# A two-layer trunk: the second matrix product of both MLPs in another order of work

## The chip, the cores and the metric

One core of one Trainium2 chip runs the whole kernel as one launch. The metric is the device time of that launch in microseconds: the median of the runs of one kernel. Beside it stands one profiled execution, whose trace all views below come from.

## The reference, cut to what matters

Two layers, each a mixer and an MLP, over 1024 tokens of 1024 features. `sandwich` is put around each of the four sublayers; the MLPs are sublayers 1 and 3, and sublayer 3 is the last of the kernel.

```python
def rms_norm(x, w=None):
    y = x32 * lax.rsqrt(jnp.mean(x32 * x32, axis=-1, keepdims=True) + EPS)
    ...
def squared_relu_mlp(h, w1, w2):                 # w1: 1024 x 4096, w2: 4096 x 1024
    return jnp.square(jax.nn.relu(h @ w1)) @ w2

def sandwich(x, c_act, sublayer, g_pre, g_post, w_mod, b_mod):
    shift, scale, gate = jnp.split(c_act @ w_mod + b_mod, 3, axis=-1)
    h = rms_norm(x, g_pre) * (1 + scale[:, None]) + shift[:, None]
    return x + gate[:, None] * rms_norm(sublayer(h), g_post)
```

All of it is float32. The kernel makes each float32 product from three products of a shorter format: each operand is split into a high part (a cast) and a low part (what the cast left), and high x high, high x low and low x high are added.

## The kernel before

The MLP (`mlp`, L492) works in two stages. The first product (loop L590) makes the hidden activations feature by feature and stores seven combinations of their quarters to DRAM (`ud[1]` to `ud[7]`, each 16 feature tiles of 128 x 512). The second product multiplies them with combinations of the four quarters of `w2` (x11, x12, x21, x22; each 2048 x 512). It is a Strassen-Winograd scheme: seven products of half size in place of eight, and additions. The results are four quarters of the output: `top` holds the first 512 tokens (row tiles 0 to 3), `low` the last 512 (row tiles 4 to 7), each with two halves of 512 columns.

Before the change the second product (L655 to L736) is cut in two passes `c` over the features. A pass loads eight feature tiles of all four quarters of `w2` into SBUF (L676, 1 MB per load, in the four large buffers hh0, hl0, hh1, hl1). Then it makes the seven products in the order 1, 2, 5, 3, 6, 4, 7. A product takes four PSUM banks, one per row tile, and four steps `q` of two feature tiles; a step forms the difference of weights where needed (L684 to L689, VectorE), splits the weights (`split_w`: high part on ScalarE L156, low part on VectorE L158; a ring of four buffers) and the activations (`split_to`, L489 and L490; buffers from a ring of six), and issues 24 matmuls of 512 columns (L701 to L703). After a product's four steps the banks are emptied: in the first pass by a copy on ScalarE (L706), in the second by an addition on VectorE (L709), with the scheme's further additions behind it (L711 to L722).

A finished row tile goes through `post` (L384): squares summed on ScalarE (L390), the gain `gg` by GpSimd in two halves (L393; by VectorE for every fourth tile), reciprocal root (L133 on VectorE, L135 on GpSimd), and one VectorE instruction that scales it and adds the old `x` (L398), with a load of `x` before and a store behind. If another sublayer follows, `pre_norm` squares the new `x` (L380), and L382 normalizes it into `Y`; `hT_cols` transposes `Y` on TensorE (L414) and makes the high and low parts of the next sublayer's input (L416 to L418). Row tiles 0 to 3 are posted after product 6 of the second pass (L724), row tiles 4 to 7 after all products (L731). The next mixer begins with units that need only the first half of hT.

A scheduler orders the instructions of each engine when the kernel is built; on the chip every engine runs its own in that order. All loads and stores of this stage are issued on SyncE's queue, in order.

Of the kernel before, what the change touches and what calls it, by code (L numbers as in the profile page):

```python
# [9 lines left out]
F32 = mybir.dt.float32  # L10
F32R = mybir.dt.float32r
# [7 lines left out]
P = 128  # L19
D = 1024  # L20
# [8 lines left out]
def trunk(ctx: ExitStack, tc: tile.TileContext, x, c, rel_bias, norm_gains, mod_w, mod_b, mlp_w1, mlp_w2,  # L29
# [372 lines left out]

    def new_hT(hf):
        return tuple(hp.tile([P, 8, 512], F32R, tag=f"{n}{hf}", name=f"{n}{hf}") for n in ("hh", "hl"))
# [87 lines left out]
    def mlp(yp, s):  # L492
# [19 lines left out]
        with ExitStack() as st:  # L512
# [77 lines left out]
            for it in range(8):  # L590
# [68 lines left out]
        mid = [slot(t, pair, F32, "mid") for t in range(4)]  # L659
        five = [slot(4 + t, pair, F32, "five") for t in range(2)]  # L660
        acc = {1: [m[:, 0] for m in mid], 6: [m[:, 1] for m in mid], 2: [m[:, 0] for m in top], 3: [m[:, 1] for m in top],
               4: [m[:, 0] for m in low], 7: [m[:, 1] for m in low], 5: [five[t // 2][:, t % 2] for t in range(4)]}
# [3 lines left out]
        def u_slot():  # L666
            us_at[0] += 1
            return slot((8, 9, 10, 11, 6, 7)[us_at[0] % 6], pair, F32R, "u")

        for c in range(2):  # L670
            xs = {}
            for key, tag, j, n in ((11, "hh0", 0, 0), (21, "hl0", 1, 0), (12, "hh1", 0, 1), (22, "hl1", 1, 1)):
                xs[key] = hp.tile([P, 8, 512], F32, tag=tag, name="x")
                for h in range(2):
                    r0 = j * 2048 + c * D + h * 512
                    nc.sync.dma_start(out=xs[key][:, h * 4:h * 4 + 4],  # L676
                                      in_=w2[r0:r0 + 512, n * 512:n * 512 + 512].rearrange("(k p) n -> p k n", p=P))
            for i, key in ((1, 11), (2, 21), (5, 11), (3, 22), (6, 22), (4, 21), (7, 12)):
                ps = [bank() for _ in range(4)]
                for q in range(4):  # L680
                    ks = slice(q * 2, q * 2 + 2)
                    x11, x12, x21, x22 = (xs[k][:, ks] for k in (11, 12, 21, 22))
                    if i == 5:
                        tt(out=x11, in0=x12, in1=x11, op=sub)  # L684
                    elif i == 6:
                        tt(out=x12, in0=x22, in1=x12, op=sub)
                        tt(out=x22, in0=x22, in1=x11, op=sub)
                    elif i == 4:
                        tt(out=x21, in0=x21, in1=x22, op=sub)  # L689
                    wh, wl = split_w(pair, xs[key][:, ks])  # L690
                    if q % 2 == 0:
                        raw = wp.tile([P, 4, 512], F32, tag="raw", name="uraw", bufs=2)
                        k0 = c * 8 + q * 2
                        nc.sync.dma_start(out=raw, in_=ud[i][k0:k0 + 4].rearrange("k p n -> p k n"))
                    uh, ul = u_slot(), u_slot()
                    split_to(uh, ul, raw[:, q % 2 * 2:q % 2 * 2 + 2])
                    for t in range(4):
                        ts = slice(t * P, t * P + P)
                        for k in range(2):
                            first, last = q == 0 and k == 0, q == 3 and k == 1  # L700
                            mm(ps[t], lhsT=uh[:, k, ts], rhs=wh[:, k], start=first, stop=False)  # L701
                            mm(ps[t], lhsT=uh[:, k, ts], rhs=wl[:, k], start=False, stop=False)  # L702
                            mm(ps[t], lhsT=ul[:, k, ts], rhs=wh[:, k], start=False, stop=last)  # L703
                for t in range(4):
                    if c == 0:
                        nc.scalar.copy(out=acc[i][t], in_=ps[t])  # L706
                        continue
                    a = {n: v[t] for n, v in acc.items()}
                    tt(out=a[i], in0=ps[t], in1=a[i], op=add)  # L709
                    if i == 2:  # L710
                        tt(out=a[2], in0=a[1], in1=a[2], op=add)  # L711
                    elif i == 3:
                        tt(out=a[3], in0=a[5], in1=a[3], op=add)
                    elif i == 6:
                        tt(out=a[6], in0=a[1], in1=a[6], op=add)
                        tt(out=a[3], in0=a[6], in1=a[3], op=add)
                        tt(out=a[5], in0=a[6], in1=a[5], op=add)
                    elif i == 4:
                        tt(out=a[4], in0=a[6], in1=a[4], op=add)
                    elif i == 7:  # L720
                        tt(out=a[4], in0=a[7], in1=a[4], op=add)
                        tt(out=a[7], in0=a[5], in1=a[7], op=add)  # L722
                if c == 1 and i == 6:
                    for t in range(4):  # L724
                        x_new = post(yp, t, s, yp.Y[t])
                        if s != sub_last:
                            pre_norm(yp, t, x_new)
# [3 lines left out]
        for t in range(4):  # L731
            x_new = post(yp, 4 + t, s, slot(t, [P, D], F32, "yg"))
            if s != sub_last:
                pre_norm(yp, 4 + t, x_new)
# [802 lines left out]
```

## Time and profile before

| | us |
|---|---|
| median of three runs | 3067.3 |
| lowest and highest run | 3060.2 and 3067.34 |
| the profiled execution | 3064.09 |
| its span | 3062.1 |
| TensorE busy in the span | 2931.0 |
| VectorE busy | 2039.6 |
| ScalarE busy | 1327.1 |
| GpSimd busy | 489.0 |

The span reaches from the first to the last instruction of the core. The second product of the first MLP fills it from about 1430 to 1746 us, that of the second MLP from about 2720 to 3038 us. TensorE (PE) is matmul, PEld the load of its weights beside it, DVE is VectorE, ACT ScalarE, POOL GpSimd, SP SyncE. Busy time is a share of a stretch; what a stretch waits for is read from the bracket behind an instruction, which gives its engine's idle time just before it and who ended it.

### The profile page before, as it was taken

The numbers are of one execution on the slowest core, as the hardware profiler recorded it, in microseconds if no ns is written. First come the engines' busy times: TensorE is split into PE (matmuls) and PEld (weight loads), VectorE is DVE, ScalarE is ACT, GpSimd is POOL, SyncE is SP. The second block draws the span as 40 slices with busy tenths as digits, with TensorE's granted clock in tenths as the row PEclk, the third lists the DMA queues.
The fourth block names the chain that finished last, engine by engine and source line by source line (L and its number), as shares of the span: only waits on it lengthen the run. The fifth ranks groups of instructions, "written<-read, shape, count | busy, mean of one in ns | idle before, by whom it ended". The sixth has DMA issues, their size and how long they took to land.

```text
span 3062.1 us, 39916 instructions
## 1 busy us (share of the span) xinstructions
PE 2931.0 (96%) x15250; PEld 2471.6 (81%) x15250; DVE 2039.6 (67%) x3282; ACT 1327.1 (43%) x2372; POOL 489.0 (16%) x434
## 2 busy tenths in 40 slices
PE   8999989999999989999999889999999899999996
PEld 5878879888877868888888678989988688888885
DVE  5797885555686488867557845565454876675577
ACT  5233335555543264445443365432222654454432
POOL 0243543222200120000000432001101100000004
PEclk9999999999999999999999989999999999999998
DMA  6231312111132246647443442153232454474423
GB/s 212 74 102 56 111 48 64 48 56 49 41 146 104 76 144 242 210 143 274 138 163 97 131 126 63 32 169 110 82 139 90 138 179 165 152 268 151 151 97 124
DMA packets 250786, 380.03 MB, mean 124 GB/s; under 512 B 13801, under 2 KB 149602, under 8 KB 249698
## 3 DMA queue, kind: packets, MB, share of 16 engines
q1 hardware_dynamic: 250208, 377.36, 36.8%
q8 instruction: 120, 1.97, 0.3%
q14 instruction: 72, 0.59, 0.1%
q10 hardware_dynamic: 386, 0.11, 0.0%
HBM read 285.67 MB, written 91.75 MB: 123 GB/s over the span
## 4 chain that ended last, share of the span: by engine, by line
PE 80%; DVE 11%; DMA 4%; ACT 2%; issue 2%; POOL 1%; SPq 0%; DVEq 0%; ACTq 0%; POOLq 0%
PE pw L701 4%; PE pw L702 4%; PE pw L703 4%; PE pw L536 4%; PE pw L537 4%; PE pw L538 4%; PE pg L433 4%; PE pg L434 4%; PE pg L435 4%; PE pg L751 4%; PE pg L753 3%; PE pg L752 3%; PE pg L445 3%; PE pg L447 3%; PE pg L446 3%; PE pg L536 2%
## 5 line engine op out<-in xcount | busy, mean ns | idle before, releaser
L156 ACT CAST wh<-raw 128x1024 fp32r<-128x1024 f32 (+1 forms) x218 | 227.6, 1047 | 305.7 <-PE pw L537 99.0
L751 PE MATMUL pg<-wh,hh 128*128 128x256 f32 (+1 forms) x992 | 292.1, 295 | 15.8 <-DVE zs L786 11.4
L433 PE MATMUL pg<-hh,wh 128*128 128x512 f32 x736 | 292.1, 398 | 1.8 <-ACT hh L416 0.7
L434 PE MATMUL pg<-hl,wh 128*128 128x512 f32 x736 | 291.6, 396 | 0.5 <-DVE hl L418 0.3
L435 PE MATMUL pg<-hh,wl 128*128 128x512 f32 x736 | 291.8, 396 | 0.0
L753 PE MATMUL pg<-wh,hl 128*128 128x256 f32 (+1 forms) x992 | 287.6, 290 | 0.6 <-DVE hl L418 0.6
L752 PE MATMUL pg<-wl,hh 128*128 128x256 f32 (+1 forms) x992 | 288.0, 290 | 0.0
L158 DVE TENSOR_TENSOR wl<-raw,wh 128x1024 fp32r<-128x1024 f32 (+1 forms) x162 | 199.5, 1233 | 129.3 <-ACT wh L156 126.4
L490 DVE TENSOR_TENSOR u<-uraw,u 128x1024 fp32r<-128x1024 f32 x112 | 139.1, 1242 | 191.8 <-ACT u L489 191.0
L489 ACT CAST u<-uraw 128x1024 fp32r<-128x1024 f32 x112 | 117.2, 1048 | 311.0 <-PE pw L702 209.1
L701 PE MATMUL pw<-wh,u 128*128 128x512 f32 x608 | 241.0, 397 | 0.0
L702 PE MATMUL pw<-wl,u 128*128 128x512 f32 x608 | 240.4, 395 | 0.0
L703 PE MATMUL pw<-wh,u 128*128 128x512 f32 x608 | 239.4, 394 | 0.0
L751 PEld LDWEIGHTS pg<-wh,hh 128*128 128x128 f32 x992 | 193.6, 195 | 19.0 <-DVE zs L786 10.7
L135 POOL TENSOR_TENSOR rs<-ms,expo 128x1 f32<-128x1 f32 x160 | 108.1, 677 | 617.2 <-DVE ms L133 599.1
L753 PEld LDWEIGHTS pg<-wh,hl 128*128 128x128 f32 x992 | 193.1, 195 | 2.6 <-DVE hl L418 1.3
L752 PEld LDWEIGHTS pg<-wl,hh 128*128 128x128 f32 x992 | 193.4, 195 | 1.9 <-issue 0.5
L445 PE MATMUL pg<-wh,u 128*128 128x512 f32 x448 | 182.1, 407 | 3.6 <-DVE u L883 3.0
L393 POOL TENSOR_TENSOR top<-top,gg 128x512 f32<-128x512 f32 x12 | 29.7, 2500 | 965.2 <-ACT junk L390 965.2
L447 PE MATMUL pg<-wh,u 128*128 128x512 f32 x448 | 178.6, 399 | 0.0
L446 PE MATMUL pg<-wl,u 128*128 128x512 f32 x448 | 177.5, 396 | 0.0
L158 POOL TENSOR_TENSOR wl<-raw,wh 128x1024 fp32r<-128x1024 f32 x58 | 145.5, 2512 | 146.4 <-ACT wh L156 127.3
(462 smaller groups left out, 7443.1 us busy)
## 6 DMA issues: line engine op xcount, KB each, us to landing
uraw<-ud SPq DMA_DIRECT2D x56, 1024.0 KB, 5.4
x<-in_mlp_w_dram SPq DMA_DIRECT2D x32, 1024.0 KB, 7.4
raw<-in_mod_w_dram SPq DMA_DIRECT2D x24, 1024.0 KB, 5.0
ud<-sums SPq DMA_DIRECT2D x48, 512.0 KB, 4.3
raw<-in_mlp_w_dram SPq DMA_DIRECT2D x18, 1024.0 KB, 5.5
raw<-in_e_w_in_dram SPq DMA_DIRECT2D x32, 512.0 KB, 4.0
ud<-c SPq DMA_DIRECT2D x64, 256.0 KB, 2.5
mraw<-in_mod_w_dram SPq DMA_DIRECT2D x32, 512.0 KB, 5.1
```

Source lines behind the costliest of these rows:

```text
L158: lo_on[0].tensor_tensor(out=wl, in0=src, in1=wh.bitcast(F32), op=ALU.subtract)
L433: mm(ps, lhsT=wh[:, k], rhs=hh[:, k], start=(k == 0), stop=False)
L434: mm(ps, lhsT=wh[:, k], rhs=hl[:, k], start=False, stop=False)
L435: mm(ps, lhsT=wl[:, k], rhs=hh[:, k], start=False, stop=(k == 7))
L445: mm(ps, lhsT=uh[:, tl], rhs=wh[:, f % 2], start=(f == 0), stop=False)
L447: mm(ps, lhsT=ul[:, tl], rhs=wh[:, f % 2], start=False, stop=(f == 3))
L701: mm(ps[t], lhsT=uh[:, k, ts], rhs=wh[:, k], start=first, stop=False)
L702: mm(ps[t], lhsT=uh[:, k, ts], rhs=wl[:, k], start=False, stop=False)
L703: mm(ps[t], lhsT=ul[:, k, ts], rhs=wh[:, k], start=False, stop=last)
L751: mm(ps[:, 0:n], lhsT=hh[:, k, tl], rhs=wh[:, i], start=(k == 0), stop=False)
L752: mm(ps[:, 0:n], lhsT=hh[:, k, tl], rhs=wl[:, i], start=False, stop=False)
L753: mm(ps[:, 0:n], lhsT=hl[:, k, tl], rhs=wh[:, i], start=False, stop=(k == 7))
```

## The change

The two passes become one: each of the seven products runs over all 16 feature tiles (eight steps) in PSUM. The order is 1, 2, 6, 5, 3, 7, 4. Product 2 goes on in the banks of product 1, and product 3 in those of product 5, after a copy or an addition has read them. Per MLP 56 readings of a bank become 32, and the additions that followed them go away but for those listed.

The weights no longer lie in SBUF whole: a `Stream` loads a quarter of `w2` in eight pieces of 512 KB. W11 is kept over products 1, 6 and 5, W22 over 6 and 4; W21, W22 and W12 are loaded again for later products, W12 and the second W21 through two small buffers that take turns (`tags` is None). The ring for split activations grows from six to eight buffers.

Row tiles 0 to 3 are posted in product 7 (`finish`), and the first half of hT is made in the first half of product 4. That product's last four steps are held: their operands are split, and then their matmuls are issued row tile by row tile, 24 each, with the end of that tile behind it (`post_tail`). `half_sum` treats a half of a row tile: the square's sum on ScalarE, the gain on VectorE (first half) or GpSimd (second half, done ahead). The loads of `xt` go to buffers of their own.

```diff
+    def half_sum(yp, y, cc):
+        junk = yp.tmp.tile([P, 512], BF16, tag="junk", name="junk")
+        ss = stat.tile([P, 1], F32, tag=f"ssh{cc}", name="ssh")
+        nc.scalar.activation(junk, y, AF.Square, accum_out=ss)
+        (nc.gpsimd if cc else nc.vector).tensor_tensor(out=y, in0=y, in1=gg[:, cc * 512:cc * 512 + 512], op=ALU.mult)
+        return ss
+
+    def post_tail(yp, t, s, xt, ss1):
+        src = x[0].rearrange("(t p) d -> t p d", p=P) if s == subs[0] else xd[s - 1]
+        nc.sync.dma_start(out=xt, in_=src[t])
+        Y = yp.Y[t]
+        ss0 = half_sum(yp, Y[:, 0:512], 0)
+        nc.vector.tensor_tensor(out=ss0, in0=ss0, in1=ss1, op=ALU.add)
+        r = rstd_of(ss0, D)
+        nc.vector.scalar_tensor_tensor(out=xt, in0=Y, scalar=r, in1=xt, op0=ALU.mult, op1=ALU.add)
+        dst = out[0].rearrange("(t p) d -> t p d", p=P) if s == sub_last else xd[s]
+        nc.sync.dma_start(out=dst[t], in_=xt)
+        return xt
...
-            return slot((8, 9, 10, 11, 6, 7)[us_at[0] % 6], pair, F32R, "u")
-
-        for c in range(2):
...
-            for i, key in ((1, 11), (2, 21), (5, 11), (3, 22), (6, 22), (4, 21), (7, 12)):
...
+            return slot((8, 9, 10, 11, 4, 5, 6, 7)[us_at[0] % 8], pair, F32R, "u")
...
+            def step(self, q):
+                if self.tags is None:
+                    t = slot(2 + turn("x"), pair, F32, "x")
+                    nc.sync.dma_start(out=t, in_=self.src[q])
+                    return t
+                if q == len(self.kept):
+                    t = hp.tile([P, 4, 2, 512], F32, tag=self.tags[q // 4], name="x")
+                    for i in range(4):
+                        nc.sync.dma_start(out=t[:, i], in_=self.src[q + i])
+                        self.kept.append(t[:, i])
+                return self.kept[q]
+
+        h0, h1 = ("hh0", "hl0"), ("hh1", "hl1")
+
+        t1, t2_ = Stream(11, h0), Stream(22, h1)
+        plan = ((1, [t1]), (2, [Stream(21, h1)]), (6, [t2_, Stream(12, None), t1]), (5, [t1]), (3, [Stream(22, h0)]),
+                (7, [Stream(22, h0), Stream(12, None)]), (4, [Stream(21, None), t2_]))
...
+                if i == 4 and q >= 4:
+                    held.append((uh, ul, wh, wl))
+                else:
+                    products(ps, [(uh, ul, wh, wl)], range(4), q == 0 and i not in (2, 3), q == 7, more)
+                if i == 7 and q % 2:
+                    finish(q // 2, yp.Y[q // 2])
+                if i == 4 and s != sub_last and q < 4:
+                    if q == 0:
+                        hT[0] = new_hT(0)
+                    hT_cols(yp, 0, s + 1, hT[0], (2 * q, 2 * q + 1))
...
+            for t in range(4):
+                c11, c12, c21, c22 = top[t][:, 0], top[t][:, 1], low[t][:, 0], low[t][:, 1]
...
+                elif i == 7:
+                    tt(out=c22, in0=ps[t], in1=c22, op=add)
+                    tt(out=c21, in0=ps[t], in1=u2[t], op=add)
+                else:
+                    if t == 0:
+                        sums = [half_sum(yp, c22_, 1) for c22_ in (l_[:, 1] for l_ in low)]
+                    products(ps, held, (t,), False, True, more)
+                    tt(out=c21, in0=ps[t], in1=c21, op=add)
+                    x_new = post_tail(yp, t + 4, s, xts[t], sums[t])
+                    if s != sub_last:
+                        pre_norm(yp, 4 + t, x_new)
```

What the scheduler makes of it, first on TensorE at the end of the first MLP, before: `pht` is a bank for transposes, `top` row tiles 0 to 3, `pg<-hh,wh` a matmul of the next mixer's first unit.

```order
L702 MATMUL pw<-wl,u 128x512
L414 MATMUL pht<-kmat,top 128x128 x2
L703 MATMUL pw<-wh,u 128x512
L414 MATMUL pht<-kmat,top 128x128 x2
L433 MATMUL pg<-hh_14969,wh 128x512 x2
L414 MATMUL pht<-kmat,top 128x128 x4
L434 MATMUL pg<-hl_14970,wh 128x512
L435 MATMUL pg<-hh_14969,wl 128x512
```

The same place after the change (L740 to L742 are the product's matmuls, L435 the transposes, L454 to L456 the mixer's first unit; `low` is row tile 4):

```order
L740 MATMUL pw<-wh,u 128x512
L741 MATMUL pw<-wl,u 128x512
L742 MATMUL pw<-wh,u 128x512
L435 MATMUL pht<-kmat,low 128x128 x2
L454 MATMUL pg<-hh_14840,wh 128x512
L455 MATMUL pg<-hl_14841,wh 128x512
L456 MATMUL pg<-hh_14840,wl 128x512
```

The transposes of row tile 3 (`top`) and most of those for the first half of hT, which stood behind the last matmul and among the mixer's first unit, are among the matmuls of product 4 now; behind the last matmul stand two transposes of an earlier tile and the mixer's units.

On VectorE at the end of the kernel, before (numbers of buffers kept: low_23535 is row tile 7):

```order
L709 TENSOR_TENSOR low_23535<-pw_25497,low_23535 128x512
L721 TENSOR_TENSOR low_23534<-low_23534 128x512
L721 TENSOR_TENSOR low_23535<-low_23535 128x512
L133 TENSOR_SCALAR ms_25662<-ss_25658 128x1
L722 TENSOR_TENSOR low_23534<-five_23541,low_23534 128x512
L722 TENSOR_TENSOR low_23535<-five_23541,low_23535 128x512
L393 TENSOR_TENSOR yg_25684<-low_23535,gg_106 128x512
L398 SCALAR_TENSOR_TENSOR xt_25652<-yg_25642,rs_25650,xt_25652 128x1024
```

After (low_23524 and low_23525 are row tiles 6 and 7, L788 reads their banks):

```order
L788 TENSOR_TENSOR low_23524<-pw_25316,low_23524 128x512
L408 TENSOR_TENSOR low_23524<-low_23524,gg_106 128x512
L417 TENSOR_TENSOR ssh_25631<-ssh_25631,ssh_25523 128x1
L133 TENSOR_SCALAR ms_25635<-ssh_25631 128x1
L419 SCALAR_TENSOR_TENSOR xt_25512<-low_23524,rs_25637,xt_25512 128x1024
L788 TENSOR_TENSOR low_23525<-pw_25317,low_23525 128x512
L408 TENSOR_TENSOR low_23525<-low_23525,gg_106 128x512
L417 TENSOR_TENSOR ssh_25668<-ssh_25668,ssh_25527 128x1
L133 TENSOR_SCALAR ms_25672<-ssh_25668 128x1
L419 SCALAR_TENSOR_TENSOR xt_25513<-low_23525,rs_25674,xt_25513 128x1024
```

Before, all four last tiles were read, combined and scaled together behind the last matmul; now a tile is done whole before the next one's bank is read.

On VectorE between products 7 and 4 of the first MLP, after the change (pw_14405 and pw_14406 are product 7's banks of row tiles 4 and 5; `wl` the low part of a weight split):

```order
L511 TENSOR_TENSOR u_14923<-uraw_14920,u_14922 128x1024
L782 TENSOR_TENSOR low_12975<-pw_14405,low_12975 128x512
L783 TENSOR_TENSOR low_12975<-pw_14405,u2_12979 128x512
L158 TENSOR_TENSOR wl_14918<-x_14913,wh_14916 128x1024
L731 TENSOR_TENSOR x_14968<-x_14968,x_13545 128x1024
L782 TENSOR_TENSOR low_12976<-pw_14406,low_12976 128x512
L783 TENSOR_TENSOR low_12976<-pw_14406,u2_12979 128x512
```

Before, between products 4 and 7 of the second pass:

```order
L490 TENSOR_TENSOR u_15086<-uraw_15051,u_15085 128x1024
L709 TENSOR_TENSOR low_12975<-pw_14821,low_12975 128x512
L158 TENSOR_TENSOR wl_15115<-x_13999,wh_15113 128x1024
L382 TENSOR_SCALAR top_12971<-xt_14746,rs_14755 128x1024
L398 SCALAR_TENSOR_TENSOR xt_14767<-top_12972,rs_14765,xt_14767 128x1024
L709 TENSOR_TENSOR low_12976<-pw_14822,low_12976 128x512
L719 TENSOR_TENSOR low_12975<-mid_12979,low_12975 128x512
```

A bank was freed by one addition and is freed by two, with a split and a difference between two row tiles.

## Rows read from the trace of the kernel before

**Rows 1.** The page, parts 1 and 2: busy us by engine; TensorE's granted clock.

```profile
PE 2931.0 (96%) x15250; PEld 2471.6 (81%) x15250; DVE 2039.6 (67%) x3282; ACT 1327.1 (43%) x2372; POOL 489.0 (16%) x434
...
PEclk9999999999999999999999989999999999999998
```

**Rows 2.** Stretches: length, busy us (instructions) by engine, granted clock, DMA share, GB/s.

```profile
1430.00:1746.60 316.60, 316.60 (x1364) 255.95 (x1363) 215.11 (x213) 132.94 (x156) 24.51 (x15) 1.00 0.44 149
1746.60:1764.50 17.90, 0.02 (x1) 0.00 (x0) 17.74 (x20) 3.40 (x6) 11.01 (x8) 0.58 0.38 123
1764.50:1798.00 33.50, 29.12 (x144) 23.75 (x145) 22.28 (x34) 28.91 (x46) 8.66 (x10) 0.82 0.57 189
1798.00:1845.00 47.00, 46.43 (x242) 39.20 (x241) 15.38 (x29) 21.73 (x33) 16.35 (x9) 1.00 0.25 71
2735.00:3037.90 302.90, 302.88 (x1301) 244.53 (x1299) 202.28 (x197) 122.93 (x140) 21.44 (x12) 1.00 0.40 136
3037.90:3062.10 24.20, 0.02 (x1) 0.00 (x0) 14.54 (x17) 3.91 (x8) 10.94 (x9) 0.61 0.36 130
```

**Rows 3.** Timeline, TensorE, first MLP's end: start, us, line, count, [idle before, releaser].

```profile
1746.14 0.47 PE L703 MATMUL pw<-wh,u 128*128 128x512 f32 x1
1764.55 0.69 PE L414 MATMUL pht<-kmat,top 128*128 128x128 f32 x2 [17.94 <-DVE top L382]
...
1788.09 0.58 PE L751 MATMUL pg<-wh,hh 128*128 128x256 f32 x1 [1.30 <-DVE qk L1228]
...
1793.38 1.22 PE L414 MATMUL pht<-kmat,low 128*128 128x128 f32 x8
1794.35 0.37 PE L751 MATMUL pg<-wh,hh 128*128 128x256 f32 x1
...
1797.90 0.29 PE L753 MATMUL pg<-wh,hl 128*128 128x256 f32 x1
```

**Rows 4.** Timeline, VectorE, the same place.

```profile
1762.75 1.75 DVE L382 TENSOR_SCALAR top<-xt,rs 128x1024 f32<-128x1024 f32 x1
...
1768.91 0.15 DVE L133 TENSOR_SCALAR ms<-ss 128x1 f32<-128x1 f32 x1 [0.34 <-ACT junk L380]
1769.80 0.75 DVE L382 TENSOR_SCALAR low<-xt,rs 128x1024 f32<-128x1024 f32 x1 [0.73 <-POOL rs L135]
```

**Rows 5.** Timeline, TensorE and VectorE, end of the kernel.

```profile
3037.53 0.40 PE L703 MATMUL pw<-wh,u 128*128 128x512 f32 x1
...
3056.89 1.28 DVE L398 SCALAR_TENSOR_TENSOR xt<-yg,rs,xt 128x1024 f32<-128x1024 f32 x1 [0.95 <-DMA xt<-xd]
```

**Rows 6.** Groups by line, 1427 to 1746: count, busy us, mean ns, idle before.

```profile
L490 DVE TENSOR_TENSOR u<-uraw,u 128x1024 fp32r<-128x1024 f32 x55 | 68.2, 1240 | 94.5 <-ACT u L489 94.5
...
L709 DVE TENSOR_TENSOR low<-pw,low 128x512 f32<-128x512 f32 x3 | 2.0, 682 | 0.0
...
L390 ACT ACTIVATE junk<-top 128x1024 bf16<-128x1024 f32 x4 | 4.2, 1043 | 0.0
...
L706 ACT COPY low<-pw 128x512 f32<-128x512 f32 x5 | 2.9, 580 | 1.4 <-PE pw L703 1.4
...
L390 ACT ACTIVATION_READ_ACCUMULATOR junk<-top 128x1 f32 x4 | 0.7, 187 | 0.0
```

**Rows 7.** Timeline, GpSimd and VectorE, first MLP, while GpSimd applies the gain.

```profile
1704.17 6.50 POOL L393 TENSOR_TENSOR top<-top,gg 128x512 f32<-128x512 f32 x2 [371.06 <-ACT junk L390]
...
1707.78 1.73 DVE L715 TENSOR_TENSOR mid<-mid 128x512 f32<-128x512 f32 x1
```

**Rows 8.** DMA: two stretches as in rows 2; two loads, median us to landing.

```profile
2.00:32.00 30.00, 20.76 (x81) 9.30 (x82) 16.13 (x40) 12.77 (x21) 2.42 (x6) 0.89 1.00 322
...
1427.00:1457.00 30.00, 30.00 (x130) 24.28 (x129) 27.18 (x30) 16.59 (x23) 0.00 (x0) 1.00 1.00 368
...
x<-in_mlp_w_dram SPq DMA_DIRECT2D x32, 1024.0 KB, 7.4
...
braw<-in_mod_w_dram SPq DMA_DIRECT2D x16, 512.0 KB, 6.7
```

More of the change, by code (lines that the diff above doesn't have):

```diff
@@ L658, in mlp @@
         low = [slot(12 + t, pair, F32, "low") for t in range(4)]
[L659 to L662, printed above, removed]
+        u2s = [slot(t, pair, F32, "u2") for t in range(2)]
+        u2 = [u2s[t // 2][:, t % 2] for t in range(4)]
         yp.Y = [t.rearrange("p a n -> p (a n)") for t in top + low]
@@ L667, in u_slot @@
             us_at[0] += 1
-            return slot((8, 9, 10, 11, 6, 7)[us_at[0] % 6], pair, F32R, "u")
-        for c in range(2):
[L671 to L677, printed above, removed]
-            for i, key in ((1, 11), (2, 21), (5, 11), (3, 22), (6, 22), (4, 21), (7, 12)):
-                ps = [bank() for _ in range(4)]
[L680 to L727, printed above, removed]
-                if c == 1 and i == 4 and s != sub_last:
-                    hT[0] = new_hT(0)
-                    hT_cols(yp, 0, s + 1, hT[0], range(8))
@@ new lines, in products @@
+        def products(ps, parts, ts_, first, last, on):
+            for t in ts_:
+                ts = slice(t * P, t * P + P)
+                for n, (uh, ul, wh, wl) in enumerate(parts):
+                    for k in range(2):
+                        b, e = first and n == 0 and k == 0, last and n == len(parts) - 1 and k == 1
+                        mm(ps[t], lhsT=uh[:, k, ts], rhs=wh[:, k], start=b, stop=False, **on)
+                        mm(ps[t], lhsT=uh[:, k, ts], rhs=wl[:, k], start=False, stop=False, **on)
+                        mm(ps[t], lhsT=ul[:, k, ts], rhs=wh[:, k], start=False, stop=e, **on)
@@ new lines, in mlp @@
+        ps = xts = None
+        for i, streams in plan:
+            if i not in (2, 3):
+                ps = [bank() for _ in range(4)]
+            held, more = [], dict(skip_group_check=True) if i in (2, 3) else {}
+            for q in range(8):
+                wh, wl = split_w(pair, operand(i, [st_.step(q) for st_ in streams], q))
+                if q % 2 == 0:
+                    raw = wp.tile([P, 4, 512], F32, tag="raw", name="uraw", bufs=2)
+                    nc.sync.dma_start(out=raw, in_=ud[i][q * 2:q * 2 + 4].rearrange("k p n -> p k n"))
+                uh, ul = u_slot(), u_slot()
+                split_to(uh, ul, raw[:, q % 2 * 2:q % 2 * 2 + 2])
+                if i == 4 and q >= 4:
[8 more added lines that the diff above has]
+                    hT_cols(yp, 0, s + 1, hT[0], (2 * q, 2 * q + 1))
+            if i == 4:
+                xts = [slot(t, [P, D], F32, "xt") for t in range(4)]
+            for t in range(4):
+                c11, c12, c21, c22 = top[t][:, 0], top[t][:, 1], low[t][:, 0], low[t][:, 1]
+                if i == 1:
+                    nc.scalar.copy(out=u2[t], in_=ps[t])
+                elif i == 2:
+                    nc.scalar.copy(out=c11, in_=ps[t])
+                elif i == 6:
+                    tt(out=u2[t], in0=ps[t], in1=u2[t], op=add)
+                elif i == 5:
+                    tt(out=c22, in0=ps[t], in1=u2[t], op=add)
+                elif i == 3:
+                    tt(out=c12, in0=ps[t], in1=u2[t], op=add)
+                elif i == 7:
[7 more added lines that the diff above has]
+                    x_new = post_tail(yp, t + 4, s, xts[t], sums[t])
+                    if s != sub_last:
+                        pre_norm(yp, 4 + t, x_new)
```

22 lines of the change are left out of this document (18 added, 4 removed).

## The prediction, made before the result was known

> **What bounds the kernel now.** I read the busy shares first: TensorE is busy for 2931 of 3062 us, nearly always at full clock [rows 1]. A change can save what TensorE loses, or cut its work. This one cuts none: each MLP's second product has 7 products x 16 feature tiles x 4 row tiles x 3 matmuls = 1344 before and after.
>
> So the next view is the table by stretch [rows 2]. Inside the second product TensorE has no gap: 316.6 of 316.6 us in the first MLP (1364 matmuls, 0.232 us each), 302.88 of 302.90 in the second. DMA moved 149 and 136 GB/s there, VectorE was busy for about two thirds. What the old order costs stands behind the last matmul: 17.9 us with an idle TensorE, then 33.5 us with another 4.4 us idle at a mean clock of 0.82; in the second MLP 24.2 us up to the end of the kernel.
>
> The timeline of TensorE tells who is late [rows 3]. The last matmul of the product starts at 1746.14. The next instruction, a transpose for hT, waits 17.94 us for L382 on VectorE, the normalization of row tile 3. In those 17.9 us VectorE is busy for 17.74: it works off the seven-way sums (L719 to L722) and the posts of all tiles at once, and its L382 for row tile 3 runs from 1762.75 to 1764.5 [rows 4]. At 1788.09 the engine waits 1.30 us more, for a bank that VectorE has to read, and the 24 short matmuls from there take 5.3 us, to 1793.38, at half clock (1.2 GHz); from 1794.35 on one takes 0.12 us. At the end of the kernel the last matmul ends at 3037.93, the last VectorE instruction at 3058.17, the span at 3062.1 [rows 5].
>
> **The change part by part.**
>
> *The first MLP's end.* From 1746.14 to the matmul at 1797.90 are 51.9 us. Counted in the order, TensorE does in them 48 matmuls of 512 columns (48 x 0.232 = 11.1 us), 54 of 256 (54 x 0.12 = 6.5) and 42 transposes (an estimate of 0.11 each, from 0.12 for a short matmul: 4.6). That is 22.2 us of work; 29.7 us are lost, 22.3 by waiting [rows 2] and 7.4 by the half clock. After the change the 32 transposes for hT's first half stand among the matmuls of product 4 (they cost what they cost now, 26 of them are only moved), and behind the last matmul stand at once two whole units of the next mixer that need nothing from the last tiles: 11.1 us, then 24 short matmuls (2.9 us), and only then the transposes of the last row tile, 14 us after the last matmul.
>
> What must be done for the last tile in these 14 us: L788 (0.68, as L709), half a square on ScalarE (0.6, between L706's 0.58 and half of L390's 1.04, plus 0.19 to read the sum), the gain (0.68), the sum and rstd (0.14 + 0.89, from 1768.91 to 1769.80), L419 (1.28), square 1.23, rstd 0.89, L382 0.75 [rows 4 to 6]. That is 8.0 us with nothing in the queue before it, so it fits. But the engines run in order: the order of VectorE puts six weight splits between these steps, and `qk`, which must free the first unit's bank for the third unit, behind the last L419. I take one wait of 4 us there plus 2.4 us of half clock, the loss seen at 1788.09 (5.3 us instead of 24 x 0.12 = 2.9): 6.4 us, with 0 and 12 as ends. Gain: 29.7 - 6.4 = **23.3 us** (18 to 30).
>
> *The kernel's end.* Now each row tile's last 24 matmuls (5.6 us) run while the tile before it is finished, and the loads of `xt` are issued ahead. After the last matmul only one tile is left: 0.68 + 0.79 + 0.68 + 0.14 + 0.89 + 1.28, about 0.4 for five hand-overs, and 3.9 from the end of the last VectorE instruction to the end of the span [rows 4 to 6]. That is 8.8 us in place of 24.2: **15.4 us** gained (13 to 16). A tile before it needs some 5 us and has 5.6.
>
> *Evictions and sums.* Per MLP ScalarE loses 20 of 28 copies, VectorE 36 of 60 additions of 0.68 us. Apart from the tail both were hidden under TensorE, so I count nothing for them.
>
> *What is more densely packed.* Products 7 and 4 of the first MLP take 2 x 8 x 24 x 0.232 = 89 us of TensorE. VectorE then has 35 instructions of 1.24 us (splits and differences), 22 of about 0.68 (additions, gains, the low parts of hT), four L398 and four L382 [rows 4 to 6]: 66 us. Ten GpSimd products with the gain run beside them, and the trace shows what that does: while GpSimd needed 6.50 us for two of them, L715 took 1.73 us, where an addition of this size takes 0.68 [rows 6, 7]. Ten such delays of 1.05 make 77 of 89 us. The split tiles are up to four steps ahead, so that the margin holds on average; but product 4's third and fourth accumulators lie in banks that product 7 frees only with two additions per tile, and these stand behind a split and its wait. I take 4 us of TensorE idle (0 to 15). It is the term that I know least.
>
> *Transfers.* The weights are loaded twice: 32 MB per MLP in place of 16. Products 6 and 7 need three 512 KB pieces per step of 5.6 us, 282 GB/s. The trace moved 368 GB/s for 30 us at the start of this stage, and 322 GB/s with 512 KB pieces at the start of the kernel [rows 8]; TensorE never waited. I count nothing. What covers this is the ring of four split buffers. The change halves the size of a weight transfer, and the Trainium skill (DMA: Bandwidth & Descriptors, section Bandwidth) speaks against that: it wants transfers batched to 1 MiB or more and lists 341 GB/s for 1 MB and 138 GB/s for 64 KB. By its lower figure the estimate is 11.4 us per step and a kernel that is slower by far; by its upper one nothing changes. The 322 GB/s of [rows 8], with several 512 KB pieces in flight, says that here the size of one transfer isn't what limits.
>
> *Sum*, against the profiled execution (3064.1 us, between the lowest and the highest of the three runs and 3.2 below their median): -23.3 - 15.4 + 4 = -34.7, that is **3029 us**.
>
> **The rivals.**
> 1. *VectorE starves the second product.* In product 7 of the first MLP it could wait at each of the four row tiles for GpSimd's two gain products, 1.0 us of power and L398: about 9 us a tile if nothing overlaps. 77 + 36 = 113 us against 89 is 24 us of idle TensorE, and at the rate of [rows 2] (7.4 us of slow clock for 22.3 of idle) 32 us: 3029 + 32 - 4 = 3057 us, no change that can be told. For it: VectorE's 17.74 of 17.9 us after 1746. Against it: TensorE had no gap while the same posts ran before 1746 [rows 2], and the order puts splits between the steps.
> 2. *The first end's gain is given back.* If the next mixer is held by ScalarE and VectorE (the second half of hT) as long as before, the end of the kernel alone counts: 3064 - 15.4 + 4 = 3053 us. Against it: after 1798 TensorE is busy for 46.4 of 47 us at full clock [rows 2].
> 3. *Slower: the streams don't keep up.* The pieces of W12 have only two buffers. Gains of 38.7 us are used up when each of the 32 steps of products 6 and 7 lasts 1.2 us longer, that is at 232 GB/s or less. At the rate of one 1 MB load by itself (7.4 us [rows 8], 142 GB/s) a step lasts 11.1 us: 32 x 5.5 = 176 us more, 3202 us. For it: a DMA that waits for its buffer holds up all behind it on SyncE. Against it: 368 GB/s above. The batching rule of the Trainium skill (the page and section named above) would lead to this time, by its lower figure; it has no chance beyond this rival's.
>
> **How the numbers follow.** Forecast 0.80, rival 1 0.07, rival 2 0.08, rival 3 0.05. The forecast's own ends are the sums of its bounds: -30 - 16 + 0 gives 3018, -18 - 13 + 15 gives 3048. The range takes in rival 2 in part: 3016 to 3050. What counts as no change is 0.3%, about 9 us, which is what a measurement of this kernel can tell. Faster: 0.80 + 0.08 = 0.88; same 0.07; slower 0.05.
>
> **What would show it.** In the changed profile: TensorE without a gap of over 1 us through products 1 to 3 of both MLPs; behind the first MLP's last matmul the next mixer's units at once and no wait near 18 us; from the last matmul to the end of the span about 9 us; weight loads of 512 KB with up to 282 GB/s. I am wrong if TensorE waits for `wl` or for a bank in products 7 and 4 (rival 1), for `x` or `wh` behind DMA in products 6 and 7 (rival 3), or if the wait moves to the mixer's third unit and is much longer than 4 us (rival 2).

## The result, and the profile after

The changed kernel takes 3029.7 us (median of four runs, 3027.9 to 3030.9) beside 3066.5 us for the kernel before in the same set of runs: a ratio of the means of 0.9884, with a 95% interval of 0.9867 to 0.9901. The forecast was 3029 us. Its time came out right, and two of its terms were off by 3 to 4 us in opposite directions. The profiled execution after took 3030.93 us; its span is 3029.1 us. In a later set of runs (r_after below) one run of the changed kernel took 5505.7 us at a lower granted clock, and it is left out of that set's median.

The page, parts 1 and 2 of the changed kernel, as in [rows 1]:

```profile
PE 2929.4 (97%) x15250; PEld 2471.4 (82%) x15250; DVE 1991.2 (66%) x3222; ACT 1309.4 (43%) x2348; POOL 474.2 (16%) x430
...
PEclk9999999999999999999999999999999999999999
```

TensorE does the same 15250 instructions in nearly the same busy time. VectorE has 60 instructions and 48 us less. What changed the time must be mainly idle time of TensorE, so the next view is the table by stretch, as in [rows 2]: both second products, the two stretches behind the first one with the first 4.6 us of the second of them by themselves, and the end of the kernel.

```profile
1425.90:1750.80 324.90, 324.90 (x1416) 262.80 (x1414) 215.52 (x218) 144.86 (x176) 30.86 (x26) 1.00 0.61 214
...
1750.80:1769.70 18.90, 11.82 (x55) 9.35 (x54) 12.24 (x17) 8.06 (x12) 2.71 (x3) 0.94 0.76 241
1769.70:1802.00 32.30, 30.95 (x182) 27.57 (x183) 14.17 (x20) 20.13 (x32) 12.83 (x9) 0.93 0.31 92
...
1769.70:1774.30 4.60, 4.58 (x21) 4.60 (x22) 0.76 (x1) 0.00 (x0) 0.55 (x1) 0.50 0.82 251
...
2718.00:3021.00 303.00, 303.00 (x1302) 244.46 (x1300) 191.91 (x180) 116.45 (x133) 24.14 (x17) 1.00 0.58 201
3021.00:3029.10 8.10, 0.03 (x1) 0.00 (x0) 2.89 (x5) 0.72 (x2) 0.55 (x1) 0.66 0.31 129
```

Inside the second products TensorE is busy for every microsecond, as before. Behind the first one it now works for 11.8 of the first 18.9 us, where before it did nothing for 17.9. The last line is the kernel's end: 8.1 us in place of 24.2.

The timeline of TensorE at the end of the first MLP, answering [rows 3]:

```profile
1750.43 0.39 PE L742 MATMUL pw<-wh,u 128*128 128x512 f32 x1
1750.66 0.38 PE L435 MATMUL pht<-kmat,low 128*128 128x128 f32 x2
1750.80 0.48 PE L454 MATMUL pg<-hh,wh 128*128 128x512 f32 x1
...
1761.57 0.39 PE L456 MATMUL pg<-hh,wl 128*128 128x512 f32 x1
1761.80 0.38 PE L435 MATMUL pht<-kmat,low 128*128 128x128 f32 x2
1762.98 0.44 PE L435 MATMUL pht<-kmat,low 128*128 128x128 f32 x2 [0.80 <-DVE ms L133]
1769.72 0.55 PE L808 MATMUL pg<-wh,hh 128*128 128x256 f32 x1 [6.30 <-DVE ms L133]
1770.07 0.42 PE L809 MATMUL pg<-wl,hh 128*128 128x256 f32 x1
...
1774.34 0.29 PE L808 MATMUL pg<-wh,hh 128*128 128x256 f32 x1
```

The next mixer's two units start 0.4 us after the start of the product's last matmul and run through to 1761.8. Then the third unit waits for 6.30 us, and its matmuls go at half clock (granted clock 0.50, which is 1.2 GHz; 0.21 us each) until 1774.34. The releaser named, L133, is a small instruction that ended just before. The wait is for the bank that the first unit filled, and `qk` (L1285) frees it. VectorE at that place:

```profile
1764.56 1.28 DVE L419 SCALAR_TENSOR_TENSOR xt<-low,rs,xt 128x1024 f32<-128x1024 f32 x1 [0.44 <-POOL rs L135]
1765.76 1.22 DVE L158 TENSOR_TENSOR wl<-raw,wh 128x1024 fp32r<-128x1024 f32 x1
1768.88 0.69 DVE L1285 TENSOR_TENSOR qk<-pg,rope 128x512 f32<-128x512 f32 x1 [1.90 <-DMA rope<-in_k_rope_dram]
```

So `qk` came behind the last row tile's L419, and then 1.90 us later still, for a load. SyncE's queue shows when that load was issued:

```profile
1762.22 0.34 SPq L310 DMA_DIRECT2D gg<-in_mod_b_dram  x1
1763.00 0.34 SPq L1278 DMA_DIRECT2D rope<-in_k_rope_dram  x1
```

The next gain `gg` may be loaded only when row tile 7 has used the old one (L408 at 1761.50). The rope load stands behind it in the queue, and its buffer held the old x of row tile 6 until L382 had read it, from 1762.18 to 1762.93. Of the two conditions the buffer is the one that ended last.

To place gains I use two distances in every trace: **D**, from the first matmul of the first MLP to the first matmul of the second MLP, and **E**, from the end of the last matmul to the end of the span. For the changed kernel D lies between these two rows of TensorE's timeline:

```profile
1098.54 0.40 PE L557 MATMUL pw<-hh,wh 128*128 128x512 f32 x1
...
2372.07 0.39 PE L557 MATMUL pw<-hh,wh 128*128 128x512 f32 x1
```

and for the kernel before:

```profile
1097.23 0.40 PE L536 MATMUL pw<-hh,wh 128*128 128x512 f32 x1
...
2391.07 0.40 PE L536 MATMUL pw<-hh,wh 128*128 128x512 f32 x1
```

D fell from 1293.8 to 1273.5 us (-20.3), E from 24.2 to 8.1 (-16.1). That is 36.4 us; the two spans differ by 33.0. The missing 3.4 us are 1.3 before the first MLP and 2.1 in the first product of the second, which the change does not touch. Both stretches vary by some microseconds between the kernels below: 1096.2 to 1101.2 us up to the first MLP, 646.5 to 651.2 from the second MLP's first matmul to its last. The medians differ by 36.8.

### The profile page after: what moved, and what is told of

It reads as the page before. It is cut to its first block, busy times and chain, and to the rows that moved or that the text cites. A ratio compares the mean times of both kernels' runs of the same rounds, so it can differ in the third digit from the quotient of the medians.

```text
span 3029.1 us, 40060 instructions
## 1 busy us (share of the span) xinstructions
PE 2929.4 (97%) x15250; PEld 2471.4 (82%) x15250; DVE 1991.2 (66%) x3222; ACT 1309.4 (43%) x2348; POOL 474.2 (16%) x430
## 4 chain that ended last, share of the span: by engine, by line
PE 81%; DVE 10%; DMA 4%; ACT 2%; issue 2%; POOL 1%; SPq 0%; POOLq 0%; DVEq 0%; ACTq 0%
PE pw L740 5%; PE pw L741 5%; PE pw L742 5%; PE pw L557 4%; PE pg L454 4%; PE pg L456 4%; PE pg L455 4%; PE pw L558 4%; PE pw L559 4%; PE pg L808 4%; PE pg L809 3%; PE pg L810 3%; PE pg L466 3%; PE pg L468 3%; PE pg L467 3%; PE pg L740 2%
## 5 line engine op out<-in xcount | busy, mean ns | idle before, releaser
L454 PE MATMUL pg<-hh,wh 128*128 128x512 f32 x736 | 292.8, 398 | 1.4 <-DVE ks L1340 0.8
L456 PE MATMUL pg<-hh,wl 128*128 128x512 f32 x736 | 291.9, 397 | 0.3 <-DVE ms L133 0.3
L740 PE MATMUL pw<-wh,u 128*128 128x512 f32 x608 | 240.1, 396 | 0.0
L742 PE MATMUL pw<-wh,u 128*128 128x512 f32 x608 | 239.4, 394 | 0.0
L808 PEld LDWEIGHTS pg<-wh,hh 128*128 128x128 f32 x992 | 193.8, 195 | 21.9 <-DVE zs L843 10.3
L454 PEld LDWEIGHTS pg<-hh,wh 128*128 128x128 f32 x736 | 139.1, 189 | 29.5 <-PE pg L456 1.2
```

The source lines that it names most:

```text
L454: mm(ps, lhsT=wh[:, k], rhs=hh[:, k], start=(k == 0), stop=False)
L456: mm(ps, lhsT=wl[:, k], rhs=hh[:, k], start=False, stop=(k == 7))
L740: mm(ps[t], lhsT=uh[:, k, ts], rhs=wh[:, k], start=b, stop=False, **on)
L808: mm(ps[:, 0:n], lhsT=hh[:, k, tl], rhs=wh[:, i], start=(k == 0), stop=False)
```

## The experiments

Every kernel is the changed kernel with one edit, except where another is named. All times are medians; the ratio is one of means, to the kernel before in the same set of runs.

| kernel | us | ratio, 95% interval | D | E |
|---|---|---|---|---|
| before | 3066.5 | | 1293.8 | 24.2 |
| changed | 3029.7 | 0.9867 to 0.9901 | 1273.5 | 8.1 |
| changed, again (r_after) | 3030.5 | 0.9865 to 0.9898 | 1273.5 | 8.1 |
| e1_no_tail | 3036.6 | 0.9887 to 0.9920 | 1279.8 | 11.1 |
| e2_ht_late | 3033.9 | 0.9881 to 0.9911 | 1274.0 | 8.1 |
| e3_rope_free | 3025.3 | 0.9853 to 0.9882 | 1267.1 | 8.1 |
| e3 again (r_rope_free) | 3024.7 | 0.9850 to 0.9880 | 1266.2 | 8.1 |
| e4_evict_back | 3029.9 | 0.9870 to 0.9899 | 1273.6 | 8.1 |
| e5_pieces_256k | 3029.1 | 0.9869 to 0.9902 | 1272.5 | 8.1 |
| e6_adds_in_tail | 3040.0 | 0.9899 to 0.9929 | 1280.7 | 11.2 |
| e7_ht_late_rope_free | 3029.5 | 0.9868 to 0.9897 | 1273.8 | 8.1 |
| e8_before_no_last_sums | 3047.4 | 0.9927 to 0.9956 | 1283.4 | 15.8 |
| e10_adds_behind_7 | 3039.4 | 0.9891 to 0.9924 | 1280.0 | 9.3 |

D and E say more than the medians where an edit is worth a few microseconds: the two runs of the changed kernel agree in D within 0.1 us, those of e3 within 0.9, while the median of the kernel before moved by 2.1 (3064.6 to 3066.7) between the sets of runs.

### The product's end without the split into row tiles

```diff
-                if i == 4 and q >= 4:
-                    held.append((uh, ul, wh, wl))
-                else:
-                    products(ps, [(uh, ul, wh, wl)], range(4), q == 0 and i not in (2, 3), q == 7, more)
+                products(ps, [(uh, ul, wh, wl)], range(4), q == 0 and i not in (2, 3), q == 7, more)
...
-                    products(ps, held, (t,), False, True, more)
```

> One part of the change is undone: product 4 runs all eight steps over all four row tiles, no matmuls are held, and the ends of row tiles 4 to 7 follow one after another behind the product; the single pass, the streams and the early transposes stay. Theory A (the split of the product's end into row tiles is what shortens both ends): VectorE has four tiles to work off behind the product, about 4 x 2.9 us (0.69 + 0.69 + 0.15 + 0.15 + 1.28), less the 4 us by which the first tile's matmuls end earlier. So some 13 to 15 us from the last matmul to the end of the span instead of 8.1, and the next mixer's third unit waits about 5 us longer in the first MLP: 3040 us (3035 to 3046). Rival B (the ends are shorter because fewer additions and posts are left behind the product; the split itself hides nothing more): within 3 us of the changed kernel, 3030 us.

3036.6 us: D +6.2, E +3.0. Theory A holds, with a smaller price at the end than it said (11.1 us against 13 to 15). The window behind the last matmul:

```profile
3024.00:3035.10 11.10, 0.00 (x0) 0.00 (x0) 7.12 (x13) 0.87 (x4) 4.05 (x4) 0.60 0.46 190
```

VectorE has 7.12 us of work left there, 2.89 in the changed kernel. The split is worth 7 us by the medians and 9 by D and E, of the 37; most of the gain must come from something else.

### The 12 last sums of the kernel before

```diff
-                    elif i == 4:
-                        tt(out=a[4], in0=a[6], in1=a[4], op=add)
-                    elif i == 7:
-                        tt(out=a[4], in0=a[7], in1=a[4], op=add)
-                        tt(out=a[7], in0=a[5], in1=a[7], op=add)
```

> The kernel before, leaving out the 12 additions per MLP that the scheme makes behind products 4 and 7 of the second pass (lines 719, 721 and 722); the output lacks these sums, everything else stands. Theory A (what kept VectorE busy for 17.74 of the 17.9 us behind the first MLP's last matmul were these sums, with the posts; the new order has one addition per tile there): lines 721 and 722 take 9.9 us there, so the first end becomes 8 to 12 us shorter and the kernel's end 5 to 8: 3047 to 3053 us. Rival B (posts and transposes alone hold the next mixer, the sums fit beside them): 3063 to 3066 us.

3047.4 us, as theory A said: D -10.4, E -8.4 against the kernel before (E a little more than the 5 to 8 it named). The wait of 17.94 us at [rows 3] halves; TensorE's timeline in this kernel:

```profile
1746.55 0.40 PE L703 MATMUL pw<-wh,u 128*128 128x512 f32 x1
1756.01 0.69 PE L414 MATMUL pht<-kmat,top 128*128 128x128 f32 x2 [9.07 <-DVE top L382]
```

So these sums cost the kernel before about half of what the change gained. Eight of the twelve (L721 and L722) stood behind the first MLP's last matmul, 9.9 us of VectorE's 17.74; in the new order one addition per row tile is left there. The other four (L719, which the prediction counts there too) ran 11 to 20 us before it, and the scheduler's order of VectorE changed with the edit; the share of each line is not separated.

### Additions put back: in the middle, behind product 7, and in the tail

In the middle (ScalarE's copy, then three additions of VectorE, per bank of products 2, 6 and 3):

```diff
+                back = [nc.scalar.copy(out=c21, in_=ps[t])] + [tt(out=c21, in0=y, in1=c21, op=add) for y in (ps[t], c21, c21)] if i in (2, 6, 3) else []
```

> The changed kernel with work put back that the change took away: after products 2, 6 and 3 each of the four banks is also copied by ScalarE, added once by VectorE out of PSUM and twice within SBUF, into a part of the output buffer that is overwritten later; 12 copies and 36 additions per MLP, 24.5 us of VectorE each (0.68 us an addition). Theory A (these were hidden under TensorE and their removal gained nothing): 3030 us, within 3, and TensorE without a gap in the second product. Rival B (VectorE's time is on the path, the gain came from the additions that went away): up to 2 x 24.5 = 49 us more, 3055 to 3079 us.

3029.9 us, D and E unchanged: theory A. Both second products in this kernel:

```profile
1430.00:1751.70 321.70, 320.48 (x1392) 258.35 (x1391) 229.36 (x245) 146.54 (x180) 35.26 (x24) 1.00 0.59 207
2700.00:3019.50 319.50, 319.50 (x1372) 257.55 (x1371) 227.33 (x233) 132.09 (x157) 24.97 (x17) 1.00 0.60 211
```

VectorE does 36 instructions more per MLP, 3294 in the kernel beside 3222, and is busy for 16 us more than in the changed kernel's window of the first MLP (213.6 of 320.8 us); TensorE loses 1.2 us in the first MLP (the theory said no gap) and nothing in the second.

Behind product 7 (three instructions per bank):

```diff
-                    tt(out=c22, in0=ps[t], in1=c22, op=add)
+                    tt(out=c22, in0=ps[t], in1=c22, op=add); [tt(out=c22, in0=c22, in1=c22, op=ALU.max) for _ in range(3)]
```

> The changed kernel with three more VectorE instructions of an addition's size (a maximum of a block with itself, no value changed) behind the reading of each bank of product 7: 12 per MLP, 8.2 us, at the place where the prediction feared that VectorE starves the second product (it is busy for 38.7 of 44.7 us in product 7 and 37.1 of 48.4 in product 4 of the first MLP). Theory A (splits run ahead far enough, idle time of VectorE takes them up): within 3 us of the changed kernel, 3027 to 3033 us, no gap of TensorE over 1 us in products 7 and 4. Rival B (VectorE is at its limit there, each microsecond more stops TensorE): 8 us per MLP, 3046 us.

3039.4 us: the time of neither theory. TensorE has no gap in products 7 and 4 (first two lines), as A said; the loss is behind the product, D +6.5 and E +1.2:

```profile
1657.90:1702.40 44.50, 44.50 (x192) 35.95 (x192) 38.85 (x42) 24.56 (x32) 17.57 (x14) 1.00 0.58 193
1702.40:1753.80 51.40, 51.40 (x239) 41.92 (x238) 44.44 (x54) 25.96 (x40) 24.71 (x9) 1.00 0.45 148
...
3028.20:3037.50 9.30, 0.04 (x1) 0.00 (x0) 4.15 (x7) 0.72 (x2) 1.10 (x2) 0.61 0.43 174
```

VectorE is busy for 44.4 of 51.4 us in product 4. The scheduler also mixed the held matmuls differently: row tile 4's bank was read at 1745.74, some 8 us before the last matmul, where it was 13.5 in the changed kernel, so the ends of the row tiles are bunched. What of the 8 to 10 us for both MLPs is VectorE's time and what that order, this run does not tell.

In the tail (two instructions per row tile):

```diff
-                    tt(out=c21, in0=ps[t], in1=c21, op=add)
+                    tt(out=c21, in0=ps[t], in1=c21, op=add); [tt(out=c21, in0=c21, in1=c21, op=ALU.max) for _ in range(2)]
```

> The changed kernel with two more VectorE instructions of an addition's size (a maximum of a block with itself, which changes no value) behind the reading of each of row tiles 4 to 7 in product 4: 8 per MLP, 5.4 us of VectorE, where the run with 36 more additions behind products 2, 6 and 3 cost nothing. Theory A (VectorE's work counts where it stands behind the last matmul, and only the last tile's part of it): 2 x 0.68 = 1.4 us more at each end, 3031 to 3034 us. Rival B (a tile before the last does not fit into the 5.6 us of the next tile's matmuls, so that all four tiles' additions pile up): 5.4 us at each end, 3040 us. Rival C (hidden as well): 3030 us.

3040.0 us: rival B's time, with another split (D +7.2, E +3.1, not 5.4 each). The matmuls of product 4 stand as in the changed kernel; behind them TensorE waits three times; the last tile's transposes stand ahead of the third unit in this order:

```profile
1768.59 0.69 PE L435 MATMUL pht<-kmat,low 128*128 128x128 f32 x2 [5.97 <-DVE ms L133]
1773.58 0.69 PE L435 MATMUL pht<-kmat,low 128*128 128x128 f32 x2 [4.30 <-DVE low L382]
1776.25 0.55 PE L808 MATMUL pg<-wh,hh 128*128 128x256 f32 x1 [1.98 <-DVE qk L1285]
```

That order alone is not the cost: in e4 TensorE's instructions behind the product stand in the same order, and its D is the changed kernel's. What differs is when VectorE reaches the last tile's L382: at 1772.78, 22.2 us after the start of the last matmul, and in e4 17.2 us after it (the places of the weight splits in VectorE's order differ too). Eight instructions of 0.68 us per MLP in the tail (5.4 us) cost 7.2 us in the first MLP and 3.1 at the end, 10.3 in all; 36 additions and 12 copies per MLP in the middle cost nothing.

### The rope tables in buffers of their own

```diff
-                xts = [slot(t, [P, D], F32, "xt") for t in range(4)]
+                xts = [slot(t, [P, D], F32, "xt") for t in (0, 1, 18, 19)]
```

> The changed kernel, but the old x of row tiles 6 and 7 goes to two buffers that are free by then, instead of those into which the next mixer loads its rope tables. The order that the scheduler makes of it has both rope loads ahead of the last two stores, and VectorE's first qk before the last row tile's gain. Theory A (the 6.3 us wait before the mixer's third unit is the late rope load, queued on SyncE behind the load of gg and held by the shared buffer): the wait falls under 1 us, with it some 2 us of half clock: 3021 to 3024 us. Rival B (ScalarE's late weight loads, for which it waited 7.5 us, hold the unit as well): the wait stays at 4 us or more with another releaser, 3028 to 3030 us.

3025.3 us, D -6.4. TensorE's timeline at the same place, and below it the stretch as in the table:

```profile
1750.35 0.39 PE L742 MATMUL pw<-wh,u 128*128 128x512 f32 x1
...
1761.72 0.38 PE L435 MATMUL pht<-kmat,low 128*128 128x128 f32 x2
1761.85 0.36 PE L808 MATMUL pg<-wh,hh 128*128 128x256 f32 x1
1762.29 0.28 PE L808 MATMUL pg<-wh,hh 128*128 128x256 f32 x1
...
1750.70:1769.70 19.00, 19.00 (x119) 17.00 (x118) 14.42 (x20) 9.86 (x16) 6.37 (x5) 1.00 0.69 215
```

No wait and no half clock: theory A, though the time is 1.3 us above its range. VectorE still waited 2.80 us for ScalarE's late splits in this run, and the third unit did not care: rival B falls. Two things changed at once, though: the loads are issued at 1725.8 and 1733.0 instead of 1763.0 and 1771.7, and with the loads early the scheduler put `qk` ahead of the last row tile's gain. Their shares are not separated. The second pair of runs:

> The changed kernel again, beside the version with free buffers on the same chip and with the same runs of the kernel before: 3028 to 3032 us, ratio 0.987 to 0.990.

> The version with free buffers for the old x of row tiles 6 and 7, again. If its gain over the changed kernel is real: 3023 to 3027 us, 4 to 6 us less than the changed kernel in the same set of runs, a ratio lower by 0.0013 to 0.002. If it came from one set of runs alone: within 2 us of the changed kernel.

3030.5 and 3024.7 us: the gain stands. This version is the fastest of all, 0.9865 of the kernel before (0.9850 to 0.9880).

### The first half of hT made late

```diff
-                if i == 4 and s != sub_last and q < 4:
-                    if q == 0:
-                        hT[0] = new_hT(0)
-                    hT_cols(yp, 0, s + 1, hT[0], (2 * q, 2 * q + 1))
...
+        hT[0] = make_hT(yp, 0, s + 1)
```

> One part of the change is undone: the 32 transposes for the first half of hT, with their copies, come behind product 4 instead of in its first half; the rest of the change stays. Theory A (the place of hT is a part of the first end's gain): 3.5 us of transposes come back behind the last matmul, and ScalarE needs 8 x 1.5 = 12.3 us for the copies, in which the mixer's first unit has 5.5 us of work, so that TensorE waits some 7 us; a part of it takes the place of the 6.3 us wait before the third unit. 3038 us (3033 to 3044), and the end of the kernel as in the changed kernel (8.1 us). Rival B (the mixer is held by its third unit alone, whatever stands before it): 3030 us, within 2.

3033.9 us, within theory A's range, but D only +0.5, so theory A's 8 us are refuted at the place it named. The 32 transposes behind the product and the short waits for their copies filled the time in which the third unit waited anyway: its wait is 2.20 us instead of 6.30, and it starts at nearly the same moment as in the changed kernel (1769.72):

```profile
1769.84 0.39 PE L808 MATMUL pg<-wh,hh 128*128 128x256 f32 x1 [2.20 <-DVE qk L1285]
```

Why the median is 4.2 us higher stays open: in its profiled execution, 2.4 us above the changed kernel's, 2.6 us lie in the second MLP's first product, which the edit does not touch (one wait of 2.4 us for VectorE there is not in the changed kernel). With both edits:

> Two edits together: the free buffers for the old x of row tiles 6 and 7 (which alone gave 3025.3 us) and the transposes for the first half of hT behind product 4 (alone 3033.9 us, with a first MLP's end as long as in the changed kernel). Theory A (late transposes were hidden under the wait for the third unit, which was there anyhow; without that wait their 3.5 us and the copies of ScalarE show): 3 to 7 us more than with the free buffers alone, 3028 to 3032 us. Rival B (the place of the transposes does not matter, the copies are fast enough): 3025 us, within 2.

3029.5 us, D +6.7 against e3: theory A. With the rope tables out of the way the early transposes are worth 4 us by the medians and 7 by D. Not all of it is the transposes' own time, as the theory had it, since a wait for `qk` is back, which VectorE reaches later in this order:

```profile
1767.65 0.39 PE L808 MATMUL pg<-wh,hh 128*128 128x256 f32 x1 [2.94 <-DVE qk L1285]
```

### Smaller weight loads

```diff
-                    nc.sync.dma_start(out=t, in_=self.src[q])
+                    [nc.sync.dma_start(out=t[:, k], in_=self.src[q][:, k]) for k in range(2)]
...
-                        nc.sync.dma_start(out=t[:, i], in_=self.src[q + i])
+                        [nc.sync.dma_start(out=t[:, i, k], in_=self.src[q + i][:, k]) for k in range(2)]
```

> The changed kernel with every streamed weight piece loaded as two loads of 256 KB (one feature tile each, rows of the same length) instead of one of 512 KB; bytes and buffers as before. Theory A (with several loads in flight the size of one does not limit, and the streams run far ahead): 3030 us, within 3, TensorE without a gap in the second product. Rival B (the smaller the load the lower the rate; the Trainium skill, DMA: Bandwidth & Descriptors, section Bandwidth, wants 1 MiB or more): if halving a load halved the rate, from the 346 GB/s of product 1 in the changed kernel to 173, each of the 16 steps of products 6 and 7 would last 9.1 us instead of 5.6: 56 us per MLP, some 3140 us.

3029.1 us, TensorE without a gap: theory A. The first MLP's second product in this kernel:

```profile
1430.00:1750.80 320.80, 320.80 (x1397) 259.47 (x1396) 214.24 (x216) 142.59 (x172) 30.82 (x26) 1.00 0.61 211
```

## Point by point

**The first MLP's end** (forecast 29.7 lost before, 6.4 left). D says -20.3 where the forecast's two terms for this stretch sum to -23.3 + 4 = -19.3. The mechanism was right: no wait near 18 us, the mixer's units at once, one wait before the third unit, for the bank that `qk` reads behind the last L419. The term that was mis-sized is "one wait of 4 us there plus 2.4 us of half clock". Measured are 0.80 and 6.30 and two of about 0.25 us, 7.6 in all, and about 2.0 us of half clock (some 21 matmuls of 0.21 instead of 0.12): 9.6. Of the 6.30 us, 1.90 are VectorE's wait for the rope load; without it some 4.4 would be left (an estimate), near the 4 that the step took for the order of VectorE. So what the step lacked is the load and the three short waits. The row for the load is not on VectorE but on SyncE: which loads does the third unit's releaser need, and what holds them back? The new buffers of `xt` were also those of the rope tables. e3 takes that away, and with it the late place of `qk` in the order, and gets 6.4 us back.

The prediction's listed steps of the last tile add up to 7.3 us, not to 8.0; either fits into its 14 us. In the trace the last tile's L382 starts at 1770.37, 19.9 us after the start of the last matmul, with weight splits and `qk`'s wait in between.

**TensorE idle in products 7 and 4** (forecast 4, 0 to 15): 0. The estimate of VectorE's load, 77 of 89 us, was close: 38.7 and 37.1 us in windows of 44.7 and 48.4. These are products 1, 6, 3, 7 and 4 of the first MLP in the changed kernel:

```profile
1425.90:1478.90 53.00, 53.00 (x229) 42.86 (x228) 36.95 (x38) 25.69 (x31) 0.00 (x0) 1.00 0.91 346
...
1523.60:1568.30 44.70, 44.70 (x193) 36.10 (x192) 20.77 (x19) 16.50 (x17) 0.00 (x0) 1.00 0.29 95
...
1613.00:1657.70 44.70, 44.70 (x193) 36.11 (x193) 30.31 (x28) 17.16 (x18) 0.77 (x1) 1.00 0.82 280
1657.70:1702.40 44.70, 44.70 (x193) 36.10 (x193) 38.70 (x42) 24.02 (x32) 18.14 (x15) 1.00 0.57 190
1702.40:1750.80 48.40, 48.40 (x228) 39.41 (x227) 37.06 (x47) 27.31 (x42) 11.96 (x12) 1.00 0.45 153
```

A busy share of 0.87 did not stop TensorE; that the splits run ahead is the likely reason, not a tested one. Rival 1 is refuted as written. But the margin is not large: e10's 8.2 us more per MLP, with the order that came with them, cost 6.5 in the first MLP and 1.2 at the end, only not as a gap in the product but behind it.

**The kernel's end** (8.8 us forecast, 15.4 gained): 8.1 and 16.1. The chain of the last tile, on VectorE, behind the last matmul at 3020.65:

```profile
3021.07 0.69 DVE L788 TENSOR_TENSOR low<-pw,low 128x512 f32<-128x512 f32 x1 [0.75 <-PE pw L742]
3022.61 0.69 DVE L408 TENSOR_TENSOR low<-low,gg 128x512 f32<-128x512 f32 x1 [0.85 <-ACT junk L407]
3023.22 0.15 DVE L417 TENSOR_TENSOR ssh<-ssh 128x1 f32<-128x1 f32 x1
3023.41 0.15 DVE L133 TENSOR_SCALAR ms<-ssh 128x1 f32<-128x1 f32 x1
3024.29 1.28 DVE L419 SCALAR_TENSOR_TENSOR xt<-low,rs,xt 128x1024 f32<-128x1024 f32 x1 [0.73 <-POOL rs L135]
```

It ends at 3025.57, 3.5 us before the end of the span where the sum took 3.9; the rest of the 0.7 us is in the chain itself, where instructions overlap by some 0.1 us each, which the sum did not take off.

**Evictions and sums**: counted as nothing apart from the tail, and e4 shows that. The prediction did not say how the tail's cost divides between sums and posts; e8 puts about half of the gain down to the sums. The pieces that were measured (sums 17 to 19 us, split 7 to 9, early transposes 4 to 7) were taken out of different kernels and need not add up, and moving the posts of row tiles 0 to 3 into product 7 was not tested by itself.

**Transfers**: counted as nothing, and right. The bytes were not needed at the rate that the forecast took, though: products 6 and 7 ran at 95 and 190 GB/s, since the streams run ahead, and the peak was 346 GB/s in product 1, with 512 KB pieces. Pieces of 512 KB and of 256 KB give the same time (e5), with several loads in flight. The Trainium skill (DMA: Bandwidth & Descriptors, section Bandwidth) has the rule to batch transfers to 1 MiB or more, beside a table measured with loads that GpSimd issued. Here SyncE issues them, and these sizes do not decide the time. Rival 3 had no part: its break-even of 232 GB/s lies below the 346 that product 1 shows with TensorE busy throughout.

**Rival 2** (the gain given back in the mixer): D shows that it stays. The whole 20.3 us are still there at the second MLP's first matmul.

The forecast was right, then, by its mechanism and with luck in the size: 3.2 us too little lost at the first end and 4 too much in products 7 and 4 cancel. Together D and E gained 36.4 us where the sum has 34.7, and the 3.4 lost outside them, which no term is about, left the profiled execution 2 us above the forecast.

## What to carry to other kernels

Work of a supporting engine has a price by its place: 36 additions in the middle of a stage cost nothing, eight instructions of the same size among and behind its last matmuls, 5.4 us, cost 7.2 us in one MLP and 3.1 in the other. So choose the order of partial products such that the last one needs the least behind it, and finish it tile by tile. When an end gets shorter, list for the first instruction that waits there every input with its queue and its buffer, loads included: the buffer that the new code borrowed was the one that the next stage wanted to load into.

## What was not expected of the hardware

The time of a load hardly follows its size here. The weight loads of the first MLP's second product, and the loads of the stored activations beside them, count, KB each and median us from issue to landing, in the changed kernel:

```profile
x<-in_mlp_w_dram SPq DMA_DIRECT2D x64, 512.0 KB, 6.0
uraw<-ud SPq DMA_DIRECT2D x27, 1024.0 KB, 5.6
```

and with the smaller pieces:

```profile
x<-in_mlp_w_dram SPq DMA_DIRECT2D x128, 256.0 KB, 5.2
```

Half the size saves 0.8 us of 6.0, and loads of twice the size take 5.6. How much of such a time is a fixed cost and how much waiting beside the other loads in flight, these rows do not tell.
